# A decoder step on one core: sums of squares on VectorE, splits and the table behind the last Silu

## The chip, the cores and the metric

The kernel runs on one core of a Trainium2 chip. A core has five engines with queues of their own: TensorE (PE, matrix products into PSUM), VectorE (DVE), ScalarE (ACT), GpSimd (POOL) and SyncE (SP, which issues most DMAs). Each executes its instructions in the order in which they stand in its queue and waits at semaphores for the others. The metric is the device time of one execution in microseconds; the median of several runs counts.

## The reference

One layer of a decoder for 512 prompt tokens and 8 sample tokens, 1024 features, all in float32: two head groups (a matrix memory and a retention) with a common input and output projection, a cross-attention over 256 memory tokens with 4 heads, a SwiGLU network of width 2816, and a last norm. What the change touches is this part:

```python
x = x + cross_attn(rmsnorm(x, g_xattn), mk_mem, mv_mem, w_cq, w_co)
hf = rmsnorm(x, g_ffn)
x = x + (jax.nn.silu(hf @ w_gate) * (hf @ w_up)) @ w_down
...
y = rmsnorm(x, g_final)
```

with `rmsnorm(x, g) = x * rsqrt(mean(x*x) + EPS) * g`.

## The kernel before

Features lie on the 128 partitions in 8 blocks (KB), the 520 tokens along the columns (N; halves of 260 are H2). X holds the residual stream. Every float32 operand of a product is written as a sum of two parts, hi and lo: `split` (L188) makes hi on ScalarE and lo on VectorE, and a product takes three matmuls, hi with hi, hi with lo and lo with hi. Weights come in tiles of 128x1024 (wraw), are cast on ScalarE (whi) and split on VectorE or GpSimd (wlo); two tiles of each part are there at a time. The order of the instructions on each engine is not that of the code alone: a scheduler sets it from a timeline that it models, unless a call fixes a place. `tc.issue_after(ins)` puts what the block issues on an engine behind an instruction of that engine; `tc.keep_in_program_order(ins)` holds an instruction in its place in the code.

The attention's output projection (L1104) runs in three passes over the blocks of its input B, with w_co in pieces; a PSUM tile pwc for each of the 8 output blocks. In the last pass `residual` (L288) adds pwc to X on VectorE (L291), splits X times a gain into A (ScalarE L194, VectorE L195) and calls `square` (L295): ScalarE squares the block, GpSimd adds the squares of blocks 1 to 6 to ssq one after the other, and VectorE adds the last. Then `norm_rows` (L280): a matmul with ones sums ssq over the partitions (nrm, one for each half of the columns), and Ln, Exp and four steps on VectorE make r_bc, the factor of each token (L273 to L278).

The network's first four blocks of gate and up (PLAIN) are plain products of A, which don't wait for the norm: TensorE computes pfg and pfu, and r_bc multiplies the sum when it is evicted from PSUM (L1200, L1208). PSUM has two such tiles, so the second pfg needs the place of the first. Beside them `operands` (L1149) forms and splits the seven sums of the normed input that the Strassen scheme takes for the 18 blocks behind (loop L1212): seven products a round (pfc, pfd, two in pfa, pfe, two in pfb), with seven sums of the weights for the next round (L1169), and evictions at L1230 to L1243. Their products with Silu are FR, in float32. The first 8 blocks of FR are split into A during the rounds, the other 14 into TT: `rest_split` did this in the last round, from its product 4 on (L1250), and between the matmuls of the down projection if any were left (L1271). Tables of functions on ScalarE are loaded by an instruction of their own: Silu needs one, and LOG_EXP is a table that has both Ln and Exp.

The down projection (L1258) takes two output blocks together and then one at a time, over A and TT, and the last block in two halves of columns; `finish` (L1280) adds the last residual, forms the final norm in pieces of 260, 130 and 130 columns (CUTS), each with an Ln and an Exp, and writes the output.

Of the kernel before, what the change touches and what calls it, by code (L numbers as in the profile page):

```python
# [10 lines left out]
F32 = mybir.dt.float32  # L11
F32R = mybir.dt.float32r
I32 = mybir.dt.int32
AF = mybir.ActivationFunctionType
ALU = mybir.AluOpType
# [8 lines left out]
P = 128  # L24
D = 1024
KB = 8
T = 512
NS = 8
N = T + NS
# [3 lines left out]
NM = 256  # L33
# [10 lines left out]
LOG_EXP = "natural_log_exp_and_others"  # L44
# [9 lines left out]
V_BUF, V_WC, V_BC, V_GMIX, V_GX, V_GF, V_GM, V_GH, V_GO = 0, 24, 28, 29, 30, 31, 32, 33, 34  # L54
# [61 lines left out]
def halves(ap):  # L116
    return ap.rearrange("p (a b) -> p a b", a=2)
# [23 lines left out]
def decoder_step(ctx: ExitStack, tc: tile.TileContext, i: dict, o: list):  # L141
    nc = tc.nc
    pe, act, dve, pool, sp = nc.tensor, nc.scalar, nc.vector, nc.gpsimd, nc.sync
# [21 lines left out]
    def ps1(name):  # L165
        return psums[-1].tile([P, 512], F32, tag="msc", name=name)

    X = main.tile([P, KB, N], F32, name="X")
# [4 lines left out]
    ssq = main.tile([P, N], F32, name="ssq")  # L173
# [14 lines left out]
    def split(hi, lo, src, scale=None):  # L188

        if scale is None:  # L190
            act.copy(hi, src)  # L191
            dve.tensor_tensor(lo, src, hi.bitcast(F32), ALU.subtract)  # L192
        else:
            act.activation(hi, src, AF.Copy, scale=scale)  # L194
            dve.scalar_tensor_tensor(lo, src, scale, hi.bitcast(F32), ALU.mult, ALU.subtract)  # L195
# [37 lines left out]
    def step():  # L233

        for t in list(tasks):
            t[1] -= 1
            if t[1] <= 0:
                try:
                    t[1] = next(t[0]) or 2
                except StopIteration:  # L240
                    tasks.remove(t)
# [38 lines left out]
    def norm_rows(pl):  # L280

        for a in range(2):
            h = slice(a * H2, (a + 1) * H2)
            ps = ps1("nrm")[:, :H2]
            pe.matmul(ps, ones, ssq[:, h], start=True, stop=True)
            rsqrt_rows(pl, r_bc[:, h], ps)

    def residual(pl, ps, ob, out, g_row):  # L288

        xb = X[:, ob]  # L290
        dve.tensor_tensor(halves(xb), halves(xb), ps[:, :, :H2], ALU.add)  # L291
        split(out[:, 0, ob], out[:, 1, ob], xb, scale=vec[:, ob, g_row : g_row + 1])
        square(pl, ob)

    def square(pl, ob):  # L295
        xb = X[:, ob]
        if ob == 0:
            act.activation(ssq, xb, AF.Square)
        else:
            s = pl.tile([P, N], F32, tag="row", name="sq")  # L300
            act.activation(s, xb, AF.Square)  # L301
            (dve if ob == KB - 1 else pool).tensor_tensor(ssq, ssq, s, ALU.add)  # L302
# [513 lines left out]
    cp = cx.enter_context(tc.tile_pool(name="cp", bufs=2))  # L816
# [9 lines left out]
    KT = cp.tile([P, 2, KB, NM], F32R, name="KT", bufs=1)  # L826
    Vm = cp.tile([P, 2, 2, D], F32R, name="Vm", bufs=1)
# [273 lines left out]
    queries(2)  # L1101
    queries(3)

    for (k0, nk, nc_), need in zip(PASSES, (1, 2, 3)):  # L1104
        while min(done[0], attended[0]) < need or any(t[2] == "mem" for t in tasks):
            step()
        for c0 in range(0, D, nc_):
            hi, lo = W.get()
            for c in range(0, nc_, P):
                ob = (c0 + c) // P  # L1110
                ps = ps2("pwc")
                for k in range(nk):
                    mm_k(ps, hi, lo, B, k, k0 + k, k == 0, k == nk - 1, c0=c)
                    if k == 1 and nk > 2:
                        step()
                if k0 + nk == KB:
                    residual(rowp, ps, ob, A, V_GF)
                else:
                    xb = X[:, ob]
                    dve.tensor_tensor(halves(xb), halves(xb), ps[:, :, :H2], ALU.add)  # L1120
                step()
    norm_rows(rowp)
    cx.close()
    bpool_cm.__exit__(None, None, None)
# [10 lines left out]
    FR = fp.tile([P, FB - KB, N], F32, name="FR")  # L1135
# [7 lines left out]
    def ff(s, k, ts):  # L1143
        return A[:, s, k, ts] if k < KB else TT[:, k - KB, s, ts]
# [38 lines left out]
            yield 1  # L1183

    def ff_split(f, raw):
        split(ff(0, f, slice(None)), ff(1, f, slice(None)), raw)

    unsplit = list(range(KB, FB))

    def rest_split(n):  # L1190
        for _ in range(min(n, len(unsplit))):
            f = unsplit.pop(0)
            ff_split(f, FR[:, f - KB])

    ops = []
    for f in range(PLAIN):
        ps = proj(A, "pfg")
        gu = tp.tile([P, 4, H2], F32, tag="gu", name="gu").rearrange("p (a z) n -> p a (z n)", a=2)
# [13 lines left out]
    for f in range(PLAIN, FB):  # L1212
        last, nxt = f == FB - 1, []
        more = weight_operands(nxt) if not last else iter(())
        next(more, None)
        ab, cd = ps2("pfa"), ps2("pfb")
        pc, pd, pe_ = (ps1(z)[:, :H2] for z in ("pfc", "pfd", "pfe"))
        ps = [pc, pd, ab[:, 0, :H2], ab[:, 1, :H2], pe_, cd[:, 0, :H2], cd[:, 1, :H2]]
        gu = tp.tile([P, 4, H2], F32, tag="gu", name="gu")
        g1, g2, v1, v2 = (gu[:, z] for z in range(4))  # L1220
        for j, (out, (wh, wl), (xh, xl)) in enumerate(zip(ps, ops, xs)):
            for k in range(4):
                for w, x in ((wh, xh), (wh, xl), (wl, xh)):
                    pe.matmul(  # L1224
                        out, w[:, k * P : (k + 1) * P], x[:, k * H2 : (k + 1) * H2],
                        start=k == 0 and w is wh and x is xh, stop=k == 3 and w is wl,
                    )
            next(more, None)
            if j == 0:
                act.copy(g2, out)  # L1230
            elif j == 1:
                dve.tensor_tensor(g1, out, g2, ALU.add)
                act.activation(g1, g1, AF.Silu)
            elif j == 3:
                dve.tensor_tensor(g2, out, g2, ALU.add)
                dve.tensor_tensor(v1, ps[2], g2, ALU.add)
            elif j == 4:
                dve.tensor_tensor(gu[:, 1::2], out.unsqueeze(1).broadcast_to([P, 2, H2]), gu[:, 1:3], ALU.add)
            elif j == 6:
                dve.tensor_tensor(gu[:, 1:3], cd[:, ::-1, :H2], gu[:, 1:3], ALU.add)  # L1240
                act.activation(g2, g2, AF.Silu)
                to = FR[:, f - KB if f >= KB else f]
                dve.tensor_tensor(halves(to), gu[:, 0:2], gu[:, 2:4], ALU.mult)  # L1243
            if f - PLAIN < KB and j == 5:
                ff_split(f - PLAIN, FR[:, f - PLAIN])
            if last:
                if j == 3:
                    W.fill(1)
                if j > 3:
                    rest_split(2)  # L1250
        list(more)
        ops = nxt
    tp_cm.__exit__(None, None, None)
    tc.keep_in_program_order(act.preload_act_table_set(LOG_EXP))

    yx = ExitStack()
    yp = yx.enter_context(tc.tile_pool(name="yp", bufs=4))
    for obs in ((0, 1), *((ob,) for ob in range(2, KB - 1))):  # L1258
        pss = [ps2("pfd") for _ in obs]
        for k0 in range(0, FB, KB):  # L1260
            for ps in pss:
                hi, lo = W.get()
# [34 lines left out]
    for n0, n in ((0, H2), (H2, N - H2)):  # L1297
        ts = slice(n0, n0 + n)
        ps = ps2("pfd")[:, 0, :n]
        for k0 in range(0, FB, KB):  # L1300
            if n0 == 0:
                chunks.append(W.get())
            hi, lo = chunks[k0 // KB]
# [80 lines left out]
```

## Time and profile before

| | us |
|---|---|
| median of 3 runs | 876.3 |
| lowest and highest | 875.74, 878.33 |
| the profiled execution, its own time | 874.8 |
| its span, first to last instruction | 873.0 |
| TensorE busy | 833.0 (95%) |
| VectorE busy | 671.6 (77%) |
| ScalarE busy | 406.7 (47%) |
| GpSimd busy | 179.4 (21%) |

A timeline names an instruction by its start in the span, its duration, engine, line and tiles; what stands in brackets is how long the engine stood before it and who released it. Durations of neighbours overlap a little, so the time from one start to the next is what an instruction costs its engine. A share of busy time is a mean over stages: in the span's slices TensorE is at 0.9 or more nearly throughout, VectorE from about 500 to 730 as well, and in the last slice no engine reaches 0.5.

### The profile page before, as it was taken

The numbers are of one execution on the slowest core, as the hardware profiler recorded it, in microseconds if no ns is written. First come the engines' busy times: TensorE is split into PE (matmuls) and PEld (weight loads), VectorE is DVE, ScalarE is ACT, GpSimd is POOL, SyncE is SP. The second block draws the span as 40 slices with busy tenths as digits, with TensorE's granted clock in tenths as the row PEclk, the third lists the DMA queues.
The fourth block names the chain that finished last, engine by engine and source line by source line (L and its number), as shares of the span: only waits on it lengthen the run. The fifth ranks groups of instructions, "written<-read, shape, count | busy, mean of one in ns | idle before, by whom it ended". The sixth has DMA issues, their size and how long they took to land.

```text
span 873.0 us, 17065 instructions
## 1 busy us (share of the span) xinstructions
PE 833.0 (95%) x6707; PEld 816.0 (93%) x6707; DVE 671.6 (77%) x1512; ACT 406.7 (47%) x798; POOL 179.4 (21%) x185
## 2 busy tenths in 40 slices
PE   6989999999999999999999899999999998999992
PEld 5989989999999999889999899999999998999992
DVE  6999999877786777876888899999999996222314
ACT  5545435434546353466442655555455555222324
POOL 5554442222024300415232400000000000000100
PEclk9999999999999999999999999999999999999996
DMA  8333223333345346894764223323334331333302
GB/s 273 99 98 124 88 94 123 124 100 125 103 147 194 114 129 200 266 305 107 241 206 149 73 73 106 111 87 110 98 98 120 117 104 59 105 96 91 107 5 98
DMA packets 32680, 110.56 MB, mean 127 GB/s; under 512 B 4000, under 2 KB 6176, under 8 KB 32344
## 3 DMA queue, kind: packets, MB, share of 16 engines
q1 hardware_dynamic: 27216, 95.80, 35.0%
q0 software_dynamic: 3616, 12.34, 4.1%
q10 hardware_dynamic: 1768, 1.34, 0.5%
q8 instruction: 53, 0.87, 0.4%
q14 instruction: 27, 0.22, 0.1%
HBM read 100.38 MB, written 9.07 MB: 125 GB/s over the span
## 4 chain that ended last, share of the span: by engine, by line
PE 73%; DVE 16%; DMA 4%; ACT 3%; issue 2%; POOL 1%; SPq 0%; DVEq 0%; ACTq 0%; POOLq 0%
PE pfd L1266 13%; PE pfb L1224 6%; PE pfa L1224 6%; PE pcq L223 5%; PE pgt L223 4%; PE pwc L223 4%; PE ppl L223 4%; PE pwo L223 3%; PE pfc L1224 3%; PE pfd L1224 3%; PE prp L223 3%; PE pfe L1224 3%; PE pfu L223 2%; DVE cv L518 2%; DVE wlo L209 2%
## 5 line engine op out<-in xcount | busy, mean ns | idle before, releaser
L208 ACT CAST whi<-wraw 128x1024 fp32r<-128x1024 f32 (+1 forms) x104 | 107.2, 1032 | 174.1 <-PE pfd L1266 66.4
L209 DVE TENSOR_TENSOR wlo<-wraw,whi 128x1024 fp32r<-128x1024 f32 (+1 forms) x85 | 110.0, 1296 | 67.2 <-ACT whi L208 65.2
L302 POOL TENSOR_TENSOR ssq<-ssq,sq 128x520 f32<-128x520 f32 x18 | 28.8, 1601 | 358.6 <-ACT sq L301 353.4
L1266 PE MATMUL pfd<-TT,whi 128*128 128x260 f32 x392 | 62.8, 283 | 0.0
L191 ACT CAST qhi<-wsum 128x512 fp32r<-128x512 f32 x72 | 42.9, 620 | 40.5 <-DVE wsum L1175 26.9
L209 POOL TENSOR_TENSOR wlo<-wraw,whi 128x1024 fp32r<-128x1024 f32 x19 | 45.6, 2398 | 66.2 <-ACT whi L208 61.2
L1224 PE MATMUL pfb<-TT,qhi 128*128 128x260 f32 x288 | 52.8, 283 | 2.4 <-DVE gu L1240 2.4
L1266 PEld LDWEIGHTS pfd<-TT,whi 128*128 128x128 f32 x392 | 53.7, 188 | 0.0
L1224 PE MATMUL pfa<-TT,qhi 128*128 128x260 f32 x288 | 53.1, 282 | 0.0
L192 DVE TENSOR_TENSOR qlo<-wsum,qhi 128x512 fp32r<-128x512 f32 x72 | 48.9, 682 | 0.6 <-ACT qhi L191 0.6
L223 PE MATMUL pwc<-B,whi 128*128 128x260 f32 x256 | 43.7, 287 | 4.2 <-DVE X L291 3.0
L223 PE MATMUL ppl<-A,whi 128*128 128x260 f32 x256 | 46.3, 294 | 0.6 <-DVE up L510 0.6
L1224 PEld LDWEIGHTS pfb<-TT,qhi 128*128 128x128 f32 x288 | 44.4, 188 | 2.6 <-ACT TT L191 2.6
L223 PE MATMUL pcv<-A,whi 128*128 128x260 f32 x256 | 45.3, 293 | 0.4 <-ACT whi L208 0.4
L1224 PEld LDWEIGHTS pfa<-TT,qhi 128*128 128x128 f32 x288 | 44.3, 188 | 0.0
L223 PE MATMUL pgt<-A,whi 128*128 128x260 f32 x256 | 44.0, 287 | 0.0
L223 PE MATMUL prp<-A,whi 128*128 128x260 f32 x256 | 43.8, 287 | 0.0
L223 PE MATMUL pcq<-A,whi 128*128 128x260 f32 x256 | 42.0, 283 | 0.0
L223 PE MATMUL pwo<-B,whi 128*128 128x260 f32 x256 | 41.4, 283 | 0.0
L1224 PE MATMUL pfb<-TT,qlo 128*128 128x260 f32 x144 | 40.7, 283 | 0.0
L223 PEld LDWEIGHTS pwc<-B,whi 128*128 128x128 f32 x256 | 35.8, 188 | 5.3 <-DVE X L291 3.7
L1224 PE MATMUL pfa<-TT,qlo 128*128 128x260 f32 x144 | 40.5, 281 | 0.0
(437 smaller groups left out, 2617.5 us busy)
## 6 DMA issues: line engine op xcount, KB each, us to landing
wraw<-in_weights_dram SPq DMA_DIRECT2D x132, 512.0 KB, 3.7
kv<-in_cache_k_dram SPq DMA_DIRECT2D x16, 512.0 KB, 4.4
kv<-in_cache_v_dram SPq DMA_DIRECT2D x16, 512.0 KB, 4.4
wraw<-in_weights_dram SPq DMA_DIRECT2D x8, 384.0 KB, 3.0
X<-in_x_dram SPq DMA_DIRECT2D x2, 1040.0 KB, 6.2
Cs<-in_state_C_dram POOLq DMA_DIRECT2D x4, 512.0 KB, 4.9
out_dram<-Cs POOLq DMA_DIRECT2D x4, 512.0 KB, 3.2
Ss<-in_state_S_dram POOLq DMA_DIRECT2D x4, 512.0 KB, 3.9
```

The lines of the kernel that those rows point to most:

```text
L191: act.copy(hi, src)
L192: dve.tensor_tensor(lo, src, hi.bitcast(F32), ALU.subtract)
L208: act.copy(hi[:, :n], raw[:, :n])
L209: (pool if index in LO_ON_POOL else dve).tensor_tensor(lo[:, :n], raw[:, :n], hi[:, :n].bitcast(F32), ALU.subtract)
L223: pe.matmul(ps[:m, a, :H2], w[:, k, c0 : c0 + m], x[:, s, xk, a * H2 : (a + 1) * H2], start=first and w is hi and s == 0, stop=last and w ...
L302: (dve if ob == KB - 1 else pool).tensor_tensor(ssq, ssq, s, ALU.add)
L518: dve.scalar_tensor_tensor(cv[:, :LO], up[:, j : j + LO], wc(j), cv[:, :LO], ALU.mult, ALU.add)
L1224: pe.matmul(out, w[:, k * P : (k + 1) * P], x[:, k * H2 : (k + 1) * H2], start=k == 0 and w is wh and x is xh, stop=k == 3 and w is wl,)
L1266: pe.matmul(ps[:, a, :H2], w[:, k - k0], ff(s, k, slice(a * H2, (a + 1) * H2)), start=k == 0 and w is hi and s == 0, stop=k == FB - 1 and ...
```

## The change

Three things. In the attention's last pass `residual` no longer calls `square`; ScalarE squares each block into a place of its own (sqs, in the space of the attention's keys and values KT and Vm), and VectorE sums them: blocks 0 to 2 with 3 to 5 in one addition of 1560 columns, then four of 520. `rest_split` puts its splits behind the last Silu (on ScalarE) and behind the last product (`read`, on VectorE), those of blocks 16 to 21 in program order, and the last round no longer calls it: all 14 come in the down projection. The table LOG_EXP is loaded behind the last Silu instead of at its place in the code.

```diff
--- before.py
+++ after.py
@@ -188,8 +188,7 @@
     def split(hi, lo, src, scale=None):
 
         if scale is None:
-            act.copy(hi, src)
-            dve.tensor_tensor(lo, src, hi.bitcast(F32), ALU.subtract)
+            return act.copy(hi, src), dve.tensor_tensor(lo, src, hi.bitcast(F32), ALU.subtract)
         else:
             act.activation(hi, src, AF.Copy, scale=scale)
             dve.scalar_tensor_tensor(lo, src, scale, hi.bitcast(F32), ALU.mult, ALU.subtract)
@@ -290,7 +289,8 @@
         xb = X[:, ob]
         dve.tensor_tensor(halves(xb), halves(xb), ps[:, :, :H2], ALU.add)
         split(out[:, 0, ob], out[:, 1, ob], xb, scale=vec[:, ob, g_row : g_row + 1])
-        square(pl, ob)
+        if g_row != V_GF:
+            square(pl, ob)
 
     def square(pl, ob):
         xb = X[:, ob]
@@ -1101,6 +1101,11 @@
     queries(2)
     queries(3)
 
+
+    sqs = [cp.tile([P, 2 * KB * NM], F32, tag=t, name="sqs", bufs=1) for t in ("KT", "Vm")]
+    three = sqs[0]
+    sqs = [sqs[ob == KB - 1][:, ob % 7 * N : (ob % 7 + 1) * N] for ob in range(KB)]
+
     for (k0, nk, nc_), need in zip(PASSES, (1, 2, 3)):
         while min(done[0], attended[0]) < need or any(t[2] == "mem" for t in tasks):
             step()
@@ -1115,10 +1120,14 @@
                         step()
                 if k0 + nk == KB:
                     residual(rowp, ps, ob, A, V_GF)
+                    act.activation(sqs[ob], X[:, ob], AF.Square)
                 else:
                     xb = X[:, ob]
                     dve.tensor_tensor(halves(xb), halves(xb), ps[:, :, :H2], ALU.add)
                 step()
+    dve.tensor_tensor(three[:, : 3 * N], three[:, : 3 * N], three[:, 3 * N : 6 * N], ALU.add)
+    for z in (1, 2, 6, 7):
+        dve.tensor_tensor(sqs[0] if z < 7 else ssq, sqs[0], sqs[z], ALU.add)
     norm_rows(rowp)
     cx.close()
     bpool_cm.__exit__(None, None, None)
@@ -1183,14 +1192,18 @@
             yield 1
 
     def ff_split(f, raw):
-        split(ff(0, f, slice(None)), ff(1, f, slice(None)), raw)
+        return split(ff(0, f, slice(None)), ff(1, f, slice(None)), raw)
 
     unsplit = list(range(KB, FB))
 
     def rest_split(n):
         for _ in range(min(n, len(unsplit))):
             f = unsplit.pop(0)
-            ff_split(f, FR[:, f - KB])
+            with tc.issue_after(silu.ins), tc.issue_after(read.ins):
+                both = ff_split(f, FR[:, f - KB])
+            if f >= 2 * KB:
+                for ins in both:
+                    tc.keep_in_program_order(ins)
 
     ops = []
     for f in range(PLAIN):
@@ -1238,20 +1251,19 @@
                 dve.tensor_tensor(gu[:, 1::2], out.unsqueeze(1).broadcast_to([P, 2, H2]), gu[:, 1:3], ALU.add)
             elif j == 6:
                 dve.tensor_tensor(gu[:, 1:3], cd[:, ::-1, :H2], gu[:, 1:3], ALU.add)
-                act.activation(g2, g2, AF.Silu)
+                silu = act.activation(g2, g2, AF.Silu)
                 to = FR[:, f - KB if f >= KB else f]
-                dve.tensor_tensor(halves(to), gu[:, 0:2], gu[:, 2:4], ALU.mult)
+                read = dve.tensor_tensor(halves(to), gu[:, 0:2], gu[:, 2:4], ALU.mult)
             if f - PLAIN < KB and j == 5:
                 ff_split(f - PLAIN, FR[:, f - PLAIN])
             if last:
                 if j == 3:
                     W.fill(1)
-                if j > 3:
-                    rest_split(2)
         list(more)
         ops = nxt
     tp_cm.__exit__(None, None, None)
-    tc.keep_in_program_order(act.preload_act_table_set(LOG_EXP))
+    with tc.issue_after(silu.ins):
+        act.preload_act_table_set(LOG_EXP)
 
     yx = ExitStack()
     yp = yx.enter_context(tc.tile_pool(name="yp", bufs=4))
```

Lines below number after's code, which has L290 for before's L291, L272 to L277 for L273 to L278 and, in the gate and up part, 12 or 13 more than before.

At the norm behind the attention, TensorE first; pfg and pfu are the first plain gate and up products, nrm the sum over the partitions. Before:

```order
L223 MATMUL pfu<-A,wlo 128x260
L223 MATMUL pfu<-A,whi 128x260
L285 MATMUL nrm<-ssq,ones 128x260 x2
L223 MATMUL pfu<-A,whi 128x260 x3
L223 MATMUL pfu<-A,wlo 128x260 x2
L223 MATMUL pfu<-A,whi 128x260 x4
```

and now:

```order
L222 MATMUL pfu<-A,wlo 128x260 x2
L222 MATMUL pfu<-A,whi 128x260
L284 MATMUL nrm<-ssq,ones 128x260 x2
L222 MATMUL pfu<-A,whi 128x260 x3
L222 MATMUL pfu<-A,wlo 128x260 x2
L222 MATMUL pfg<-A,whi 128x260 x4
L222 MATMUL pfg<-A,wlo 128x260 x2
```

The norm's matmuls stood early in pfu, with 35 of its 48 matmuls behind them; now 5 are, and then comes the second pfg.

VectorE at the same place, from the last addition of the squares to the eviction of pfg into gu (wlo is the low part of a weight tile), with buffer numbers, before:

```order
L302 TENSOR_TENSOR ssq_84<-ssq_84,sq_6283 128x520
L209 TENSOR_TENSOR wlo_6382<-wraw_6379,whi_6381 128x1024
L274 TENSOR_SCALAR nrmv_6288<-nrm_6286 128x260
L276 TENSOR_TENSOR r_bc_83<-nrml_6289 128x260
L274 TENSOR_SCALAR nrmv_6298<-nrm_6296 128x260
L276 TENSOR_TENSOR r_bc_83<-nrml_6299 128x260
L277 SCALAR_TENSOR_TENSOR r_bc_83<-r_bc_83,nrmv_6288 128x260
L277 SCALAR_TENSOR_TENSOR r_bc_83<-r_bc_83,nrmv_6298 128x260
L278 SCALAR_TENSOR_TENSOR r_bc_83<-r_bc_83,nrml_6289 128x260
L278 SCALAR_TENSOR_TENSOR r_bc_83<-r_bc_83,nrml_6299 128x260
L1200 TENSOR_TENSOR gu_6374<-pfg_6325,r_bc_83 128x520
```

and now:

```order
L1130 TENSOR_TENSOR ssq_84<-sqs_5531,sqs_5532 128x520
L208 TENSOR_TENSOR wlo_6375<-wraw_6372,whi_6374 128x1024
L273 TENSOR_SCALAR nrmv_6281<-nrm_6279 128x260
L275 TENSOR_TENSOR r_bc_83<-nrml_6282 128x260
L273 TENSOR_SCALAR nrmv_6291<-nrm_6289 128x260
L276 SCALAR_TENSOR_TENSOR r_bc_83<-r_bc_83,nrmv_6281 128x260
L277 SCALAR_TENSOR_TENSOR r_bc_83<-r_bc_83,nrml_6282 128x260
L208 TENSOR_TENSOR wlo_6442<-wraw_6439,whi_6441 128x1024
L275 TENSOR_TENSOR r_bc_83<-nrml_6292 128x260
L276 SCALAR_TENSOR_TENSOR r_bc_83<-r_bc_83,nrmv_6291 128x260
L277 SCALAR_TENSOR_TENSOR r_bc_83<-r_bc_83,nrml_6292 128x260
L1213 TENSOR_TENSOR gu_6367<-pfg_6318,r_bc_83 128x520
```

A second weight split has moved in between the two halves of the norm.

VectorE from the eviction of pfu to the next weight split (FR and TT hold the Strassen sums and their low parts), before:

```order
L1208 TENSOR_TENSOR gu<-pfu,r_bc 128x520
L209 TENSOR_TENSOR wlo<-wraw,whi 128x1024
L192 TENSOR_TENSOR TT<-FR,TT 128x1040
L1157 TENSOR_TENSOR FR<-FR 128x1040
L1200 TENSOR_TENSOR gu<-pfg,r_bc 128x520
L1209 TENSOR_TENSOR FR<-gu 128x520
L192 TENSOR_TENSOR TT<-FR,TT 128x1040
L209 TENSOR_TENSOR wlo<-wraw,whi 128x1024
```

and now:

```order
L1221 TENSOR_TENSOR gu<-pfu,r_bc 128x520
L191 TENSOR_TENSOR TT<-FR,TT 128x1040
L1166 TENSOR_TENSOR FR<-FR 128x1040
L1222 TENSOR_TENSOR FR<-gu 128x520
L191 TENSOR_TENSOR TT<-FR,TT 128x1040 x2
L1213 TENSOR_TENSOR gu<-pfg,r_bc 128x520
L1167 TENSOR_TENSOR FR<-FR 128x1040
L208 TENSOR_TENSOR wlo<-wraw,whi 128x1024
```

The first weight split is the one that has moved up; the second stands behind two more steps of 1040 columns than before.

ScalarE from the last round's copy of pfc on, before:

```order
L1230 COPY gu<-pfc 128x260
L191 CAST TT<-FR 128x520 x3
L1254 ACT_TABLE_LOAD
L191 CAST TT<-FR 128x520
L191 CAST qhi<-wsum 128x512
L191 CAST TT<-FR 128x520
L208 CAST whi<-wraw 128x1024
L191 CAST TT<-FR 128x520 x3
L1233 ACT_TABLE_LOAD
L1233 ACTIVATE gu<-gu 128x260
L1241 ACTIVATE gu<-gu 128x260
```

and now:

```order
L1243 COPY gu<-pfc 128x260
L191 CAST qhi<-wsum 128x512
L207 CAST whi<-wraw 128x1024
L1246 ACTIVATE gu<-gu 128x260
L1254 ACTIVATE gu<-gu 128x260 x2
L1266 ACT_TABLE_LOAD
L191 CAST TT<-FR 128x520 x8
L207 CAST whi<-wraw 128x1024 x2
L191 CAST TT<-FR 128x520 x4
```

Splits stood around the Silus of the last round, with two table loads; now the three Silus stand together, one load behind them, and then the splits. Behind this load ScalarE's order holds no other.

## Rows read from the trace of the kernel before

**Rows 1.** Busy by stretch: PE, PEld, DVE, ACT, POOL, then clock, DMA share, GB/s.

```profile
545.00:705.00 160.00, 160.00 (x1335) 160.00 (x1335) 153.34 (x275) 80.35 (x160) 0.00 (x0) 1.00 0.35 103
705.00:735.00 30.00, 26.31 (x216) 25.72 (x215) 26.52 (x45) 20.09 (x34) 0.00 (x0) 1.00 0.31 100
```

**Rows 2.** TensorE's waits, 478 to 560: total us, times, longest.

```profile
PE pwc L223 <- DVE X L291: 3.0, 2, 2.7
```

**Rows 3.** TensorE in order of time, 478 to 520: start, us; idle before in brackets.

```profile
493.36 0.64 PE L223 MATMUL pfg<-A,whi 128*128 128x260 f32 x4
...
500.67 1.04 PE L285 MATMUL nrm<-ssq,ones 128*128 128x260 f32 x4
...
506.27 0.72 PE L223 MATMUL pfg<-A,whi 128*128 128x260 f32 x4 [0.39 <-DVE gu L1200]
...
518.69 0.64 PE L223 MATMUL pfg<-A,whi 128*128 128x260 f32 x4
```

**Rows 4.** VectorE in order of time, the attention's last pass.

```profile
481.72 0.75 DVE L195 SCALAR_TENSOR_TENSOR A<-X,vec,A 128x520 fp32r<-128x520 f32 x1
...
483.16 1.89 DVE L195 SCALAR_TENSOR_TENSOR A<-X,vec,A 128x520 fp32r<-128x520 f32 x1
...
487.31 2.16 DVE L209 TENSOR_TENSOR wlo<-wraw,whi 128x1024 fp32r<-128x1024 f32 x1
489.39 1.77 DVE L195 SCALAR_TENSOR_TENSOR A<-X,vec,A 128x520 fp32r<-128x520 f32 x1
```

**Rows 5.** GpSimd in order of time, the same stretch.

```profile
483.18 1.31 POOL L302 TENSOR_TENSOR ssq<-ssq,sq 128x520 f32<-128x520 f32 x1 [1.62 <-ACT sq L301]
```

**Rows 6.** VectorE in order of time, from the norm to the third pfg.

```profile
501.46 1.23 DVE L209 TENSOR_TENSOR wlo<-wraw,whi 128x1024 fp32r<-128x1024 f32 x1 [2.45 <-ACT whi L208]
...
505.42 0.70 DVE L1200 TENSOR_TENSOR gu<-pfg,r_bc 128x520 f32<-128x520 f32 x1
...
512.01 1.21 DVE L209 TENSOR_TENSOR wlo<-wraw,whi 128x1024 fp32r<-128x1024 f32 x1
...
517.82 1.22 DVE L209 TENSOR_TENSOR wlo<-wraw,whi 128x1024 fp32r<-128x1024 f32 x1
```

**Rows 7.** Busy by stretch, columns as in rows 1, the clock behind the engines.

```profile
48.00:50.00 2.00, 0.98 (x11) 0.92 (x12) 2.00 (x6) 0.38 (x1) 1.98 (x2) 1.00 0.17 68
50.00:54.00 4.00, 4.00 (x23) 3.98 (x21) 4.00 (x9) 2.03 (x4) 1.56 (x3) 0.57 0.00 0
```

**Rows 8.** TensorE's waits, 705 to 760.

```profile
PE pfb L1224 <- DVE gu L1240: 2.4, 1, 2.4
PE pfd L1266 <- DVE gu L1236: 1.1, 1, 1.1
```

**Rows 9.** TensorE in order of time, the down projection's start.

```profile
727.68 0.74 PE L1266 MATMUL pfd<-A,whi 128*128 128x260 f32 x4 [1.05 <-DVE gu L1236]
...
739.32 0.63 PE L1266 MATMUL pfd<-TT,whi 128*128 128x260 f32 x4
```

**Rows 10.** ScalarE's groups, 700 to the end: count, busy us, mean ns.

```profile
L191 ACT CAST TT<-FR 128x520 fp32r<-128x520 f32 x14 | 8.2, 624 | 4.3 <-PE pfc L1224 2.7 <-DVE FR L1243 1.6
```

**Rows 11.** VectorE's groups, 705 to 735.

```profile
L192 DVE TENSOR_TENSOR TT<-FR,TT 128x520 fp32r<-128x520 f32 x14 | 9.1, 691 | 1.8 <-PE pfc L1224 1.1 <-ACT TT L191 0.7
```

**Rows 12.** ScalarE's groups, 700 to the end, the table loads.

```profile
L273 ACT ACT_TABLE_LOAD x3 | 3.8, 1283 | 2.5 <-PE pn L1288 2.5
L275 ACT ACT_TABLE_LOAD x3 | 3.8, 1283 | 0.1
```

**Rows 13.** ScalarE in order of time, the first norm at the end.

```profile
850.65 1.28 ACT L273 ACT_TABLE_LOAD   x1 [2.47 <-PE pn L1288]
851.95 0.48 ACT L273 ACTIVATE nrml<-pn,vec 128x260 f32<-128x260 f32 x1
```

**Rows 14.** VectorE in order of time, the end.

```profile
857.97 0.48 DVE L1284 TENSOR_TENSOR X<-X,pfd 128x130 f32<-128x130 f32 x2
```

**Rows 15.** TensorE in order of time, behind the last projection matmul.

```profile
855.31 0.61 PE L1283 MATMUL pn<-ssq,ones 128*128 128x130 f32 x4
```

## The prediction, made before the changed kernel ran

> **What bounds the kernel now.** I read the busy time by stretch first. Through the Strassen rounds of gate and up TensorE is busy 160.00 of 160 us and VectorE 153.34 [rows 1]: TensorE is the bound there, and VectorE has 4% to spare. So microseconds that TensorE loses before 545 are not won back in the rounds, and what matters is where TensorE waits. The waits and the timelines then show three places, which are the three that the change touches.
>
> Place A, the attention's last pass and the norm behind it (478 to 519). TensorE waits 3.0 us for the residual additions X of L291 [rows 2]. The cause stands in VectorE's timeline: the low half of the split, L195, takes 0.75 us at 481.72 but 1.89 at 483.16 and 1.77 at 489.39, and a weight split 2.16 at 487.31 [rows 4] against 1.23 at 501.46 [rows 6]. The long ones begin beside a GpSimd addition of ssq, as the one at 483.18 [rows 5]: two engines that add out of SBUF hold each other up here. Then the norm: its matmul at 500.67, eviction of pfg at 505.42 for 0.70 us, and the second pfg at 506.27, which waits 0.39 for that eviction [rows 3, 6].
>
> Place B, the last Strassen round (705 to 735): TensorE is busy 26.31 of 30 us [rows 1], and waits 2.4 for L1240 and 1.1 for L1236 [rows 8], both on VectorE, which has the last splits of FR in between.
>
> Place C, the end: the table of ScalarE is loaded before every Ln and every Exp, three times at L273 and three at L275, 1283 ns each [rows 12]. They lie in the chain that ends last.
>
> **The change part by part.** Profiled execution: span 873.0, time 874.8 us; I add the terms to 874.8. The median of the runs is 876.3, 1.5 higher, and I carry that 1.5 over at the end.
>
> *A, the gain in the pass.* Six GpSimd additions go, and VectorE gets one of 1560 columns and four of 520 for its one of 520. Before the sixth residual addition VectorE loses 1.14 + 1.02 + 0.93 = 3.1 us over the undisturbed 0.75, 0.75 and 1.23 [rows 4, 6]; the new additions stand behind that point. So TensorE's 3.0 go [rows 2], and with restarts pfg begins some 3.2 us earlier, at 490.1 for 493.36.
>
> *A, what takes it back.* The norm's matmul has moved in TensorE's order. Before, 61 matmuls lie between the first of pfg and the norm, (500.67 - 493.36) / 61 = 0.120 us each [rows 3]; now 91 do, 10.9 us. The sums themselves are ready by 498 (after the last split five short steps on VectorE), so the place in the order decides: 490.1 + 10.9 = 501.0, 0.3 later than before. Behind it stand only 5 matmuls (0.6 us) instead of 35, then the second pfg, which needs the PSUM tile that the eviction frees. From norm to the end of the eviction it took 5.45 us, one weight split (the one at 501.46) included [rows 3, 6]; now that split comes before the norm and the next one stands in the middle of the chain, so I take 5.45 plus 0.2. Second pfg at 506.8, 0.5 later than before: TensorE stands 4.5 us, and the gain of 3.2 has turned into a loss of 0.5.
>
> Then the third pfg, at 518.69 [rows 3]. Its low weights were split at 517.82 [rows 6], in time. In the new order the previous weight split (512.01, 1.2 us) no longer stands between eviction and that split, but two more steps of 1040 columns do, about as long as one of 1024, 1.2 [rows 6]: 517.82 + 0.6 + 1.2 = 519.6, ready at 520.8. TensorE arrives at 518.6, has four matmuls that need the high half alone (0.5), and waits 1.7. So place A ends about 1.8 later than before, and nothing behind it gives that back [rows 1]. Bounds: -3.2 if neither wait comes, +3.5 if the clock falls as well.
>
> That clock: with TensorE busy 0.98 of the 2 us from 48 on, the granted clock was 0.57 over the next 4 us [rows 7], so most of them at 1.2 instead of 2.4 GHz, and costs (1 - 0.57) x 4 = 1.7. A stand of 4.5 us may do that again. I leave it out of the sum, since the second pfg and pfu would run late into a wait for weights that ends at 520.8 anyway. The Trainium skill (TensorE: Matmul & The Clock Gate, Part 1) says that an idle TensorE falls back to half clock and that activity releases it; by that page alone the fall would be certain and the sum 1.7 worse, which is my second rival.
>
> *B.* The 14 splits of FR leave the last round and stand behind the last Silu and the last product; one table load of two goes. TensorE's 3.5 us of listed waits [rows 8] go, with three restarts and a short wait for a cast: 30 - 26.31 = 3.7 idle [rows 1], I take -4.0 (bounds -3.0 to -4.4). What hides the splits now: the down projection's first two columns begin with the eight blocks in A, 727.68 to 739.32, 11.6 us [rows 9], before the first block of TT. Last eviction, Silu and product end about 2 us after the round; a load 1.3; eight casts at 0.624 [rows 10], overlapping to 0.54, 4.4; VectorE's last of eight (0.691 [rows 11]) and the weight split behind them: about 9.2 of the 11.6. Without that cover each further microsecond would be TensorE's. The other six blocks are needed 11.5 us later.
>
> *C.* Ln and Exp find both functions in the table that is loaded once behind the last Silu, and the order shows no load behind it. The Ln at 851.95 starts where the load of 850.65 ends [rows 13], so each of the six is worth 1.28. Of the first two, 2.57, about 2.45 count: VectorE's additions of the second half at 857.97 stood behind the first half's output [rows 14], and TensorE has those sums at about 855.4 [rows 15]. The last four are in a row, 5.1. Together -7.5 (bounds -6.5 and -7.7).
>
> The Trainium skill (ScalarE: Activation LUTs, What ACT_TABLE_LOAD costs) adds a drain of 1.38 us to each load, 2.66 for a switch. By that C would be 6 x 2.66 = 16.0 and the whole -18.2. The rows show no such gap, the Ln follows 0.02 behind its load, and the measurement decides.
>
> Sum: +1.8 - 4.0 - 7.5 = -9.7; 874.8 - 9.7 = 865.1 for the profile, 876.3 - 9.7 = 866.6 for the median.
>
> **The rivals.**
> 1. The pass keeps its gain: the norm is read in time and VectorE catches up. For it: sums ready three microseconds before the norm. Against: fixed places in two orders. A = -3.2, sum -14.7: 861.6.
> 2. TensorE's stand brings the lower clock and the lag isn't absorbed. For it rows 7; against it the wait that is there anyway, and that the wait of 2.7 within rows 2 brought none. A = +3.5, sum -8.0: 868.3.
> 3. Slower: VectorE becomes the bound of the Strassen rounds. The order of evictions, splits of A and weight splits is changed in the first rounds, VectorE enters late, and has only 6.66 of 160 us free [rows 1]. One split of 520 columns in front of a needed one holds a round up by 0.7; it decides above 9.7 / 18 = 0.54 per round, in all 18 rounds: 18 x 0.7 = 12.6, 879.2. Against it: only the first rounds differ, and 96% busy held no round up before.
> 4. The table doesn't hold and loads come back at the end: only A and B, -2.2, 874.1, no change that can be told. Against it the order.
>
> **How the numbers follow.** Forecast 0.66, rivals 0.13, 0.15, 0.03 and 0.03. A difference below 0.3%, 2.6 us, can't be told from none. Faster: 0.66 + 0.13 + 0.15 = 0.94, same 0.03, slower 0.03. The forecast's own range is its terms with A at +1.0 to +2.6 and the bounds of B and C: 876.3 - 11.1 = 865.2 to 876.3 - 6.9 = 869.4. That holds the forecast and most of rival 2. The runs before lie 2.6 apart between themselves, so I widen to 862.5 and 870.0, and leave out most of rivals 1, 3 and 4, 0.19.
>
> **What would show it.** Right: pwc without waits, second pfg standing over 4 us behind the eviction, a wait for wlo in the third pfg; the last round in 10.1 us; one load after the last Silu and none after it; last Exp and end of span 7.5 us closer to the last projection. Wrong: the rounds beginning earlier than before (rival 1); a granted clock under 1 around 507 (rival 2); waits in the rounds for qlo (rival 3); TensorE waiting for TT within 12 us after the first pfd (the cover in B is too short).

## The result, and the profile after

The changed kernel took 866.15 us in the median of 4 runs (864.43 to 868.34), the kernel before 876.25 beside it (875.74 to 878.33): ratio 0.9882, 95% interval 0.9852 to 0.9912, so 7.7 to 13.0 us faster. 866.6 was predicted. Two terms were right and the third, place A, was too small by about 1. That the median came within 0.5 us is partly luck: counted as below, the change is worth 9.03 us where 9.7 were predicted, and the 10.1 between the medians holds about 1 us of what executions differ by ahead of the change.

The profiled execution of after has its own time 868.34 and span 866.6. It can't be laid on the one of before mark by mark. The first residual addition of the attention's last pass, the last thing that both kernels do alike, starts at 479.68 in before and at 482.31 in after, so after was 2.63 us late ahead of the change's first instruction. I therefore count every mark from that addition's start: "+20" is 20 us behind it. "On before's clock" means 2.63 us less than after's own time, and a stand is a stretch in which an engine waits.

**Place A.** TensorE's waits in after, 470 to 560 (total us, times, longest):

```profile
PE pfg L222 <- DVE gu L1213: 4.8, 1, 4.8
PE pwc L222 <- DVE X L1126: 0.7, 2, 0.5
PE pwc L222 <- DVE X L290: 0.3, 1, 0.3
```

The 3.0 us of [rows 2] have become 0.3, and a stand of 4.8 before the second pfg is new. VectorE of after in order of time:

```profile
484.36 0.75 DVE L194 SCALAR_TENSOR_TENSOR A<-X,vec,A 128x520 fp32r<-128x520 f32 x1
...
488.67 1.22 DVE L208 TENSOR_TENSOR wlo<-wraw,whi 128x1024 fp32r<-128x1024 f32 x1
...
493.03 1.78 DVE L1128 TENSOR_TENSOR sqs<-sqs 128x1560 f32<-128x1560 f32 x1
...
499.94 0.70 DVE L1130 TENSOR_TENSOR ssq<-sqs 128x520 f32<-128x520 f32 x1
...
506.39 0.43 DVE L277 SCALAR_TENSOR_TENSOR r_bc<-r_bc,nrml 128x260 f32<-128x260 f32 x1
506.74 1.22 DVE L208 TENSOR_TENSOR wlo<-wraw,whi 128x1024 fp32r<-128x1024 f32 x1
507.88 0.42 DVE L275 TENSOR_TENSOR r_bc<-nrml 128x260 f32<-128x260 f32 x1
...
509.26 0.70 DVE L1213 TENSOR_TENSOR gu<-pfg,r_bc 128x520 f32<-128x520 f32 x1
...
522.82 1.22 DVE L208 TENSOR_TENSOR wlo<-wraw,whi 128x1024 fp32r<-128x1024 f32 x1
```

The long splits of [rows 4] are gone (0.75, 1.22). The sums are ready at 500.64. But a weight split now stands between the two halves of the norm (506.74), where the one of before stood ahead of the norm's steps (501.46 in [rows 6]). ScalarE's cast for that split stands between the second half's Ln and Exp as well, but that costs nothing by these rows: the Exp ends at 506.81, and VectorE comes to the second half at 507.88. TensorE of after beside it:

```profile
503.63 1.04 PE L284 MATMUL nrm<-ssq,ones 128*128 128x260 f32 x4
...
510.10 1.21 PE L222 MATMUL pfg<-A,whi 128*128 128x260 f32 x4 [4.84 <-DVE gu L1213]
```

Norm to eviction takes 509.26 - 503.63 = 5.63 us, against 505.42 - 500.67 = 4.75 before [rows 3, 6]. And behind the stand the clock falls, as the stretches show (TensorE's busy time, then the clock, DMA share and GB/s):

```profile
505.00:510.00 5.00, 0.26 (x3) 0.89 0.52 154
510.00:515.00 5.00, 4.90 (x22) 0.50 0.14 56
515.00:520.00 5.00, 5.00 (x41) 0.93 0.01 3
```

TensorE has next to nothing to do from 505 to 510, and for the next 5 us it gets 0.50, that is 1.2 GHz. From the second pfg to the first pfu behind it go 8.34 us (510.10 to 518.44), 5.97 before (506.27 to 512.24).

**Places B and C.** The stretch of the last round and the one ahead of it, columns as in [rows 1]:

```profile
545.00:705.00 160.00, 160.00 (x1335) 160.00 (x1334) 153.21 (x274) 82.37 (x164) 0.00 (x0) 1.00 0.35 106
705.00:735.00 30.00, 29.97 (x251) 29.80 (x249) 25.70 (x45) 15.82 (x29) 0.00 (x0) 1.00 0.34 102
```

TensorE is busy 29.97 of 30 us against 26.31, and no wait of it is listed from 700 to 760. The splits now stand behind the last Silu. ScalarE of after, from there and at the end:

```profile
730.05 0.42 ACT L1254 ACTIVATE gu<-gu 128x260 f32<-128x260 f32 x1 [3.58 <-DVE gu L1253]
730.49 1.28 ACT L1266 ACT_TABLE_LOAD   x1
731.78 4.33 ACT L191 CAST TT<-FR 128x520 fp32r<-128x520 f32 x8
...
851.99 0.48 ACT L272 ACTIVATE nrml<-pn,vec 128x260 f32<-128x260 f32 x1 [2.48 <-PE pn L1300]
852.50 0.42 ACT L274 ACTIVATE nrml<-nrml 128x260 f32<-128x260 f32 x1
...
858.16 0.35 ACT L272 ACTIVATE nrml<-pn,vec 128x130 f32<-128x130 f32 x1
858.54 0.31 ACT L274 ACTIVATE nrml<-nrml 128x130 f32<-128x130 f32 x1
858.76 0.35 ACT L272 ACTIVATE nrml<-pn,vec 128x130 f32<-128x130 f32 x1
859.14 0.31 ACT L274 ACTIVATE nrml<-nrml 128x130 f32<-128x130 f32 x1
```

One load, and none before any Ln or Exp [rows 12, 13]. TensorE of after at the start of the down projection, at the first block of TT, and behind the last projection matmul:

```profile
729.12 0.52 PE L1278 MATMUL pfd<-A,whi 128*128 128x260 f32 x3
...
740.64 0.63 PE L1278 MATMUL pfd<-TT,whi 128*128 128x260 f32 x4
...
856.63 0.61 PE L1295 MATMUL pn<-ssq,ones 128*128 128x130 f32 x4
```

From pn to the end: 866.6 - 856.63 = 10.0 us, against 873.0 - 855.31 = 17.7 [rows 15].

### The profile page after: what moved, and what is told of

The parts are those of the page before. It is cut to its first block, busy times and chain, and to the rows that moved or that the text cites. A ratio compares the mean times of both kernels' runs of the same rounds, so it can differ in the third digit from the quotient of the medians.

```text
span 866.6 us, 17050 instructions
## 1 busy us (share of the span) xinstructions
PE 835.5 (96%) x6707; PEld 818.7 (94%) x6707; DVE 669.9 (77%) x1516; ACT 397.9 (46%) x791; POOL 169.7 (20%) x179
## 4 chain that ended last, share of the span: by engine, by line
PE 76%; DVE 13%; DMA 4%; issue 3%; ACT 2%; POOL 1%; SPq 0%; DVEq 0%; POOLq 0%; ACTq 0%
PE pfd L1278 13%; PE pfb L1237 6%; PE pfa L1237 6%; PE pcq L222 5%; PE pwc L222 4%; PE pgt L222 4%; PE pfd L1237 3%; PE pfe L1237 3%; PE pfc L1237 3%; PE pwo L222 3%; PE pfg L222 3%; PE prp L222 3%; PE ppl L222 3%; PE pfu L222 3%; DVE cv L518 2%
## 5 line engine op out<-in xcount | busy, mean ns | idle before, releaser
L208 DVE TENSOR_TENSOR wlo<-wraw,whi 128x1024 fp32r<-128x1024 f32 (+1 forms) x85 | 108.2, 1275 | 61.1 <-ACT whi L207 59.2
L302 POOL TENSOR_TENSOR ssq<-ssq,sq 128x520 f32<-128x520 f32 x12 | 19.5, 1627 | 366.5 <-ACT sq L301 361.4
L1278 PE MATMUL pfd<-TT,wlo 128*128 128x260 f32 x196 | 39.4, 282 | 0.0
```

Of the source, the lines that this page charges most:

```text
L208: (pool if index in LO_ON_POOL else dve).tensor_tensor(lo[:, :n], raw[:, :n], hi[:, :n].bitcast(F32), ALU.subtract)
L1278: pe.matmul(ps[:, a, :H2], w[:, k - k0], ff(s, k, slice(a * H2, (a + 1) * H2)), start=k == 0 and w is hi and s == 0, stop=k == FB - 1 and ...
```

## The experiments

All numbers of this table are from the profiled execution of each kernel, counted from the first residual addition of the last pass to the start of pfg, of the norm's matmul, of the second pfg and of the third pfu, and to the end of the span. The last two columns are the median of the runs and the ratio to the kernel before on the same chip, with its 95% interval. Before had medians of 878.59, 878.52 and 878.11 beside the experiments.

| kernel | pfg | norm | pfg2 | pfu3 | end | median | ratio |
|---|---|---|---|---|---|---|---|
| before | 13.68 | 20.99 | 26.59 | 44.81 | 393.32 | 876.25 | |
| after | 10.44 | 21.32 | 27.79 | 47.66 | 384.29 | 866.15 | 0.9882 (0.9852 to 0.9912) |
| after again (e_after) | 10.44 | 21.31 | 27.79 | 47.88 | 384.29 | 866.55 | 0.9876 (0.9842 to 0.9911) |
| table alone (e_table) | 14.50 | 22.56 | 28.16 | 46.38 | 387.13 | 870.42 | 0.9908 (0.9879 to 0.9937) |
| without the squares (e_nosq) | 13.69 | 21.00 | 26.61 | 44.79 | 381.28 | 864.67 | 0.9847 (0.9822 to 0.9872) |
| squares alone (e_squares) | 10.44 | 21.32 | 27.79 | 47.13 | 395.82 | 879.90 | 1.0014 (0.9993 to 1.0035) |
| no GpSimd adds (e_noadds) | 10.45 | 17.76 | 23.36 | 41.59 | 390.08 | 874.12 | 0.9955 (0.9930 to 0.9979) |
| clock held (e_hold2) | 10.44 | 21.30 | 27.78 | 47.14 | 383.67 | 868.19 | 0.9886 (0.9849 to 0.9923) |
| wlo earlier (e_wlo) | 10.44 | 21.32 | 27.79 | 47.79 | 384.35 | 866.10 | 0.9879 (0.9841 to 0.9917) |
| both (e_hold) | 10.45 | 21.31 | 27.78 | 45.37 | 381.74 | 866.82 | 0.9871 (0.9835 to 0.9906) |
| norm after 60 (e_early2) | 10.44 | 18.39 | 23.68 | 41.86 | 378.44 | 861.44 | 0.9810 (0.9784 to 0.9837) |
| norm after 66 (e_early3) | 10.46 | 18.39 | 24.39 | 42.59 | 379.09 | 862.52 | 0.9842 (0.9804 to 0.9880) |

From the third pfu to the end, the eight executions that have both B and C take 336.37 to 336.63, so 0.3 us in that column is scatter, and I take half a microsecond as a difference. The medians carry in addition what happens ahead of the change: the addition that all is counted from starts anywhere from 478.52 to 487.06 in these twelve executions, and medians of 4 runs can't tell 2 us.

**The table alone.** The kernel before, with

```diff
-                act.activation(g2, g2, AF.Silu)
+                silu = act.activation(g2, g2, AF.Silu)
...
-    tc.keep_in_program_order(act.preload_act_table_set(LOG_EXP))
+    with tc.issue_after(silu.ins):
+        act.preload_act_table_set(LOG_EXP)
```

> The kernel before with the log-exp table load alone put behind the last Silu; splits and squares as before. Theory (parts add up, the six loads at the end are worth C = -7.5 us, -6.5 to -7.7): 876.3 - 7.5 = 868.8 us, and the tail from the last pn matmul's first row to the end shrinks from 17.7 to about 10.0 us; the last Strassen round keeps its stall of about 4 us. Rival (the early splits among the Silus bring the tables back, so that the load does not hold): two or more loads stay in the tail and the time stays above 873 us.

ScalarE's groups of this kernel, 735 to the end, hold one load at L1255, behind the last Silu; the Ln and Exp have none:

```profile
L1255 ACT ACT_TABLE_LOAD x1 | 1.3, 1283 | 0.0
L273 ACT ACTIVATE nrml<-pn,vec 128x130 f32<-128x130 f32 (+1 forms) x3 | 1.2, 393 | 2.5 <-PE pn L1289 2.5
L275 ACT ACTIVATE nrml<-nrml 128x130 f32<-128x130 f32 (+1 forms) x3 | 1.0, 349 | 0.1
```

So the table holds by this edit alone, and the rival falls. From the down projection's first matmul to the end of the span before takes 393.32 - 248.00 = 145.32, this kernel 387.13 - 249.58 = 137.55: C is -7.77. The last round still has its waits, 3.0 + 0.4 + 0.2, and the third pfu to that first matmul takes 203.2, as before. Place A is 1.57 late in this execution: the clock stood at 0.80 in 493 to 495 and 0.74 in 495 to 500, which the edit, 230 us later, can't have caused. The fall stands behind the wait of 2.7 us that [rows 2] has too, and behind which before stayed at 1.00.

**Without the squares.** The changed kernel, with its squares taken back:

```diff
-        if g_row != V_GF:
-            square(pl, ob)
+        square(pl, ob)
...
-                    act.activation(sqs[ob], X[:, ob], AF.Square)
...
-    dve.tensor_tensor(three[:, : 3 * N], three[:, : 3 * N], three[:, 3 * N : 6 * N], ALU.add)
-    for z in (1, 2, 6, 7):
-        dve.tensor_tensor(sqs[0] if z < 7 else ssq, sqs[0], sqs[z], ALU.add)
```

> The changed kernel with its squares undone: the attention's last pass squares and sums as before (GpSimd adds), table load and splits as in the changed kernel. Theory (the squares cost about 2 to 3 us, place A): B + C = -4.0 - 7.6 = -11.6, so 876.3 - 11.6 = 864.7 us, which is 1.5 to 2.5 us under the changed kernel's 866.15. Rival (the pass keeps its 3.2 us and the squares pay): 866.15 + 3.2 = 869.4 us or thereabouts, slower than the changed kernel.

B and C together are worth 381.28 - 393.32 = -12.04: C is -7.97 (137.35 from the first matmul to the end), and B is the rest. So the squares cost after 384.29 - 381.28 = 3.01 us. The median, 864.67, is where the theory put it; by the medians alone the difference to after lies within the spread.

**The squares alone.** The kernel before with the same squares put in.

> The kernel before with the squares part alone; splits and table load as before. Theory (pass 3.2 us shorter, but the norm's matmul stands behind 91 matmuls instead of 61, its evictions come 1.2 us later and TensorE stands 4.8 us before pfg2): +1.8 to +2.9 over the kernel before, 878.1 to 879.2 us, and the clock falls to about 0.5 behind that stand. Rival (the gain of the pass is kept): -3.2, 873.1 us. Second rival (what the pass gains is used up exactly): 876.3 +- 0.5 us.

By the marks this kernel is 2.32 us later than before at the third pfu and 2.50 at the end; by the median it is 1.3 slower, with an interval from -0.6 to +3.1 us, so the gain of 3.2 is not there in any case. The second rival, no change, is ruled out by the marks alone. The pass has its gain (pfg 3.24 earlier), and the second pfg stands 4.84 us here too. The clock fell less this time (0.66 in 510 to 515, 1.00 behind it), the second pfg took 7.34 us to its pfu for 8.34, and yet the third pfu starts only 0.53 earlier than in after, since a wait for wlo of 0.23 turns up (the third pfg takes 6.22 for 5.76). Two limits lie close together here, and the next three kernels take them apart.

**The clock held.** The changed kernel, with TensorE's stand filled:

```diff
+        if f == 1:
+            hold = ps1("hold")[:, :H2]
+            for n in range(40):
+                mm = pe.matmul(hold, A[:, 0, n % KB, :P], A[:, 1, n % KB, :H2], start=n == 0, stop=n == 39)
+                tc.keep_in_program_order(mm)
+        with tc.issue_after(mm.ins) if f == 1 else ExitStack():
+            ps = proj(A, "pfg")
```

and one further line that holds the third pfg's wlo behind the same steps of VectorE as in the changed kernel.

> The changed kernel with 40 spare matmuls (128x260, into a spare tile that nothing reads) in the 4.8 us in which TensorE stands before pfg2, and wlo of pfg3 kept at its place on VectorE, behind the same instructions as in the changed kernel. The clock should then stay up, and pfg2 take 5.7 us instead of 8.3. Theory (two limits that stand beside each other: VectorE's queue, which works without a pause from the evictions behind the norm to wlo, 13.6 us, and TensorE's matmuls at the fallen clock): the time does not move, since pfg3's first wlo matmul then waits about 2.3 us for wlo; within 0.7 us of the changed kernel. Rival (the fallen clock alone is what made place A worse than predicted): 2.0 to 2.5 us faster than the changed kernel.

The clock stays at 1.00 from 505 to 520, and the second pfg takes 5.98; the middle stretch, columns as above:

```profile
510.00:515.00 5.00, 5.00 (x42) 1.00 0.39 108
```

And the wait that the prediction spoke of is there, in TensorE's timeline inside the third pfg, at its first low matmul:

```profile
523.33 0.64 PE L224 MATMUL pfg<-A,whi 128*128 128x260 f32 x4
525.50 0.51 PE L224 MATMUL pfg<-A,wlo 128*128 128x260 f32 x2 [1.53 <-DVE wlo L210]
```

Of the 2.4 us won in the second pfg, 0.52 to 0.74 are left at the third pfu (47.14 against 47.66 and 47.88), 0.62 at the end. The rival wanted 2.0 or more. (The median is 1.6 above that of after beside it, which four runs each can't tell from none.)

**The weight split earlier.** The changed kernel, with one split of the Strassen operands put behind the third pfg's wlo on VectorE:

```diff
+        los[-1 - j] = split(*xs[j], x)[1]
...
+    wlo = los[weight_order().index(("w_gate", 0, KB, 2 * P, P))].ins
+    tc.add_manual_dep(los[-7].ins, wlo.name, mybir.DependencyInfo(...NoSync...), reason="order")
```

> The changed kernel with wlo of pfg3 one split (1.15 us) earlier in VectorE's queue, nothing else. Theory (two limits): TensorE at the fallen clock still ends pfu2 as late, so the time does not move, within 0.7 us of the changed kernel. Rival (VectorE's queue alone sets pfg3): 1.1 us faster.

The end comes 0.06 later, which is nothing, as the theory has it. The clock fell (0.61 in 510 to 515, 0.70 in 515 to 520) and TensorE came as late as in after.

**Both at once.** The spare matmuls without the line that holds wlo back.

> Both at once: the 40 spare matmuls in TensorE's stand, and wlo of pfg3 where the scheduler then puts it, some 2.3 us earlier in VectorE's queue than in the changed kernel. Theory (two limits, each of which hides the other): now both are gone, and the kernel is 1.8 to 2.5 us faster than the changed kernel, about 864 us, though each edit alone gave nothing. Rival (the evictions' chain behind the norm sets everything, 1.2 us late whatever follows): under 0.7 us.

No wait is left on TensorE from 500 to 560, and the end is 2.55 earlier than in after: more than the two edits gave by themselves (0.62 and -0.06). That is the mark of two limits side by side, each of which hides the other. What is left of the cost of the squares is 381.74 - 381.28 = 0.46. The medians do not show it (866.82 against 866.55, 4 runs each, spread 4 us); it rests on the marks of one execution.

**The norm earlier.** The changed kernel, with

```diff
-            mm_k(ps, hi, lo, x, k, k, n == 0, n == KB - 1)
+            with tc.issue_after(behind.ins) if behind and n >= 2 else ExitStack():
+                mm_k(ps, hi, lo, x, k, k, n == 0, n == KB - 1)
...
-        ps = proj(A, "pfu", ahead=int(f < PLAIN - 1))
+        ps = proj(A, "pfu", ahead=int(f < PLAIN - 1), behind=None if f else nrm)
```

where nrm is the norm's second matmul, so that 60 matmuls lie between pfg's first and the norm, not 91. e_early3 has `n >= 3`, 66 matmuls.

> The changed kernel with one order added: from the third block of the first pfu on, TensorE's matmuls stand behind the norm's two, so that the norm's come after 60 matmuls of pfg and pfu instead of 91. The norm's matmul then waits some 0.7 us for the sums (ready at 500.6 us in the changed kernel, 60 matmuls end at 499.9). Theory (the place of the norm's matmul is what turned the 3.2 us gain into a loss): pfg2 starts about 3 us earlier, TensorE stands under 2.5 us before it, the clock does not fall to 0.5 there, and the kernel gains 3 to 5.5 us: 861 to 863 us. Rival (the evictions behind the norm and the wait for wlo of pfg3 set the end anyway): within 1 us of the changed kernel's 866.15.

> The changed kernel with the norm's two matmuls ahead of the fourth block of the first pfu, behind 66 matmuls of pfg and pfu instead of 60 or 91. Theory (any place at which the sums are just ready keeps the gain of the pass): no wait for the sums (they are ready at about the 66th matmul), pfg2 within 0.8 us of where it starts with 60, clock up, 861 to 862.5 us. Rival (the place must be exact, since ScalarE's and VectorE's weight splits come between the norm's steps): pfg2 1.5 us or more later than with 60, and over 863.5 us.

TensorE's waits from 500 to 560 with 60 matmuls:

```profile
PE nrm L285 <- DVE ssq L1132: 0.6, 1, 0.6
PE pfu L222 <- DVE wlo L208: 0.3, 1, 0.3
```

and with 66, from 496 on:

```profile
PE pfg L222 <- DVE gu L1215: 1.2, 1, 1.2
PE pfu L222 <- DVE wlo L208: 0.3, 1, 0.3
```

The stand of 4.84 is gone, the clock is 1.00 in 505 to 520, and the ends are 5.85 and 5.20 earlier than in after. That is more than the squares cost (3.01): against the kernel without the squares they now gain 2.84 (381.28 - 378.44) and 2.19 (381.28 - 379.09), most of the 3.24 of the pass. The second pfg starts 0.71 later with 66 than with 60, not 1.5, and the ends differ by 0.65, so the place need not be exact. e_early2 beats both kernels: its interval, 0.9784 to 0.9837, lies below that of the changed kernel on either chip. (Its profiled execution was its slowest, 867.31, and 4.75 later than after ahead of the change; its other six runs took 859.66 to 863.49.) In both kernels VectorE's weight split lies ahead of all the norm's steps again, not between the halves. The norm's matmul starts at +18.39 in both, with 60 after a wait of 0.6 us for the sums, and yet all that follows is earlier with 60: from norm to eviction it takes 4.41 us, 5.15 with 66. The split waits for ScalarE's cast of the weights (whi), and that starts 0.74 us earlier with 60, at +17.63 for +18.37. In both, and in after, it starts 0.24 behind the last pair of matmuls of the first pfg (+17.39 with 60, +18.13 with 66), and in before the wait ahead of that cast is put down to pfg; with 66 six more matmuls of pfu stand among those of pfg. This is read off the rows and was not tried by itself. ScalarE and VectorE with 60:

```profile
504.69 1.05 ACT L207 CAST whi<-wraw 128x1024 fp32r<-128x1024 f32 x1 [3.23 <-issue]
...
505.77 1.23 DVE L208 TENSOR_TENSOR wlo<-wraw,whi 128x1024 fp32r<-128x1024 f32 x1 [0.37 <-ACT whi L207]
506.91 0.42 DVE L274 TENSOR_SCALAR nrmv<-nrm 128x260 f32<-128x260 f32 x1
...
509.86 0.70 DVE L1215 TENSOR_TENSOR gu<-pfg,r_bc 128x520 f32<-128x520 f32 x1
```

and with 66:

```profile
499.98 1.05 ACT L207 CAST whi<-wraw 128x1024 fp32r<-128x1024 f32 x1 [3.98 <-issue]
...
501.06 1.23 DVE L208 TENSOR_TENSOR wlo<-wraw,whi 128x1024 fp32r<-128x1024 f32 x1 [1.11 <-ACT whi L207]
502.21 0.42 DVE L274 TENSOR_SCALAR nrmv<-nrm 128x260 f32<-128x260 f32 x1
...
505.15 0.70 DVE L1215 TENSOR_TENSOR gu<-pfg,r_bc 128x520 f32<-128x520 f32 x1
```

**GpSimd's adds left out.** The kernel before, where blocks 1 to 6 are squared and not added:

```diff
-        square(pl, ob)
+        if g_row != V_GF or ob in (0, KB - 1):
+            square(pl, ob)
+        else:
+            s = pl.tile([P, N], F32, tag="row", name="sq")
+            act.activation(s, xb, AF.Square)
```

> The kernel before with GpSimd's six adds of squares in the attention's last pass left out (the squares themselves are still made; the sum holds the first and the last block only). Everything else as before. Theory (GpSimd's adds beside VectorE's splits are what lengthens these from 0.75 to about 1.9 us, and the pass waits for X behind them): all eight splits take 0.75 to 0.77 us, TensorE's wait for X falls from 3.0 to about 0.3, pfg starts 3.0 to 3.7 us earlier in the pass, and since the norm's matmul stays behind 61 matmuls the gain is kept: 3 to 3.7 us under the kernel before. Rival (the long splits come from the squares on ScalarE, or from the order on VectorE): splits of 1.8 us stay, wait 3.0, no change.

The order of the instructions on ScalarE and VectorE is that of before. VectorE's splits in the pass:

```profile
483.45 0.75 DVE L195 SCALAR_TENSOR_TENSOR A<-X,vec,A 128x520 fp32r<-128x520 f32 x1
...
484.88 1.22 DVE L209 TENSOR_TENSOR wlo<-wraw,whi 128x1024 fp32r<-128x1024 f32 x1
486.01 0.76 DVE L195 SCALAR_TENSOR_TENSOR A<-X,vec,A 128x520 fp32r<-128x520 f32 x1
```

All eight take 0.75 or 0.76, pfg starts 3.23 earlier and the end is 3.24 earlier; the median says 1.8 to 6.1 less. So it was GpSimd's adds that lengthened the splits, and before's order would have kept the gain.

## Why the prediction was right, and where it was not

**The pass, A: right.** 3.2 us were predicted and 3.24 measured, with the cause that was named (e_noadds). The sum of 3.1 left out one more long split, 1.20 at 485.57, so VectorE lost 3.5 in before; the sixth addition came 3.24 earlier (11.40 behind the first before, 8.16 now), so about 0.3 of that had cost nothing. The sums were expected to be ready at 498; they were ready at +18.33, 498.0 on before's clock. The norm's matmul, set by its place behind 91 matmuls, came 0.33 later (0.3 predicted).

**What takes it back, A: right in kind, too small by about 1.** +1.8 was predicted; at the third pfu it is 47.66 - 44.81 = +2.85, or +3.07 in the second execution, beyond the +1.0 to +2.6 of the forecast's own range. The failed step is "5.45 plus 0.2" from norm to eviction's end. I gave the weight split that moves between the norm's halves 0.2 us, and it cost 0.88 (5.63 for 4.75). The rows of VectorE split this up: from the norm's matmul to the first step it is 0.79 less (504.77 - 503.63 = 1.14, for 502.60 - 500.67 = 1.93), since the earlier split is out of the way; the new one adds 1.14 (506.74 to 507.88), since the second half's steps queue behind all of it; and the steps themselves take 0.53 more, since those of a half now follow directly on one another (0.45 to 0.47 from start to start at the end, for 0.34 where the halves take turns). That made the second pfg 1.20 late, for 0.5, and wlo of the third pfg too: ready at 524.04, 521.4 on before's clock, for 520.8. With the clock held, A is 47.14 - 44.81 = +2.33: 0.5 more than predicted, and that is the chain.

**The clock.** It fell as rival 2 has it, and was mostly absorbed as the forecast has it: of the 2.4 us that the second pfg lost, 0.5 to 0.7 went through to the third pfu. The sign that I gave for the forecast, a wait for wlo in the third pfg, did not appear in after, because at the fallen clock TensorE came to the first low matmul at 524.69, 0.65 us after wlo was ready (524.04); it appeared when the clock was held, and those 0.6 us are what holding it won. The forecast's argument that the wait of 2.7 in [rows 2] brought no fall holds for that execution only: behind the same wait the table kernel's clock fell to 0.74. A single profile would have put the whole loss down to the clock, and e_hold2 shows that this is wrong.

**B: right.** -4.0 predicted. Third pfu to the down projection: 248.00 - 44.81 = 203.19 before, 246.81 - 47.66 = 199.15 after, -4.04. No kernel here has the splits alone, but without the squares the same stretch takes 199.14. The splits' cover: wlo behind the eight splits ends 9.4 us after the first pfd (9.2 predicted), and the first block of TT is wanted after 740.64 - 729.12 = 11.5.

**C: right.** -7.5 predicted, -7.84 measured (384.29 - 246.81 = 137.48 for 145.32), -7.77 with the table alone. Six loads at 1.283 are 7.70, so all six counted in full where I had let 0.2 of them be hidden. What lies above 7.70, up to 0.27 without the squares (-7.97), is open, and it puts C just outside the bound of -7.7 that I gave. By the 2.66 us for a switch in the Trainium skill (ScalarE: Activation LUTs, What ACT_TABLE_LOAD costs) they would have been worth an estimated 16.0. No kernel here agrees with that (7.77, 7.84, 7.97); the measurement decides.

The sum: +2.85 - 4.04 - 7.84 = -9.03, which is 384.29 - 393.32, 0.7 less than forecast: the miss of 1.05 in A, less 0.34 by which C came out better. The medians gave -10.1, with 7.7 to 13.0 as its interval. Rival 3 did not come: no wait in the Strassen rounds, and VectorE at 153.21 of 160. Rival 1 did not come by itself; e_early2 makes it true (378.44 - 393.32 = -14.88, for its -14.7), by one place in the order.

## What to carry to other kernels

Time won ahead of a norm or another join is kept only if the join's own instruction moves with it: count what stands in front of it on the engine, and compare with when its operands are ready. Where a loss has two causes that end at nearly the same moment, removing either one shows little or nothing, so remove both before you call one harmless. Compare single executions from the last mark that both kernels share, not from the start of the span.

## What was not expected of the hardware

The same stand of 4.84 us before the second pfg cost different amounts in different executions: from there to the next pfu went 8.34, 8.56 and 8.47 us in after, e_after and e_wlo, but 7.34 in e_squares, and 5.98 with the stand filled. Forty spare matmuls of 260 columns, which nothing reads, kept the clock at 1.00 and delayed nothing: the second pfg started at +27.78 with them and +27.79 without.

Ahead of the change, where the kernels hardly differ, executions differ by up to 8.5 us (478.52 to 487.06 for the same addition). Part of it is TensorE's clock: after had 0.83 from 60 to 70 and again from 120 to 130, e_early2 0.83 from 50 to 60, 0.78 from 120 to 130 and 0.88 from 130 to 140, where before had 0.83 from 50 to 60 and 1.00 in the other three. What happens there, and not the change, sets how far a median of a few runs can be trusted here.
